# Mixer B's scores two chunks ahead of their transposes, and one run of six transposes divided in two

## The chip, the cores and the metric

The program runs on one core of a Trainium2 chip. The metric is the device time of one execution in microseconds. Three runs of the kernel before took 348.01, 349.36 and 349.63 us (median 349.36). The profile comes from a further execution of 348.68 us; its span, from the first instruction to the last, is 346.9 us. TensorE is called PE below, VectorE DVE, ScalarE ACT, GpSimd POOL.

## The reference, cut to what matters

One layer of a decoder trunk over 256 positions of 1024 channels, in float32. `h = rmsnorm(x)`; one wide product `h @ w_in` gives queries, keys and values of three mixers, their SiLU gates and the merge logits. The three mixers are

- A: eight heads; dilated causal windows in three groups, weighted by their softmax denominators;
- B: eight heads of block-sparse attention (one block at this length, so plain causal attention with a linear bias);
- M: four heads of attention to 256 memory tokens.

```python
p_a = (o_a * jax.nn.silu(a_gate)) @ w_branch_a[l]
p_b = (o_b * jax.nn.silu(b_gate)) @ w_branch_b[l]
p_m = (o_m * jax.nn.silu(m_gate)) @ w_branch_m[l]
g_a, g_b, g_m = jnp.split(jax.nn.sigmoid(merge_logits + b_merge[l]), N_BRANCHES, axis=-1)
merged = g_a * p_a + g_b * p_b + g_m * p_m
x = x + merged @ w_out[l]
```

and the result is `rmsnorm(x)` once more. The change touches the order of the attention work of mixers A and B, and no value.

## The kernel before

**Weight chunks.** `PLAN` lists 54 chunks of weights, numbered `i` from 0. The main loop takes them in turn. Chunk `i` is loaded three chunks ahead (L85), and two chunks ahead it is split into a high and a low part: ACT casts it to `wh` (L93), DVE subtracts to get `wl` (L94), each in two halves. A chunk's product has two halves of 24 matmuls of 128x128 by 256 columns: `wh` with the high and the low part of h (L232, L233), then `wl` (L235). Value chunks have the operands the other way round (L252 to L254). The result lands in a bank `pj`, and ACT or DVE takes it out.

**Attention steps.** Each mixer handles two heads (a pair) in steps. For mixer B (`pair_steps_b`) they are `scores` (eight matmuls into two banks `sb`, L296 and L297; then, for each head, a POOL multiplication for the bias table, two DVE scans L306 that add the bias and find the extreme, two exponentials on ACT, L312, and on DVE reciprocals L313 and normalisations L314), `trans` (six transposes on PE, three for each head, L320, and one ACT copy a head from `pt` to `ptsb`, L321), and `pv` (eight matmuls L449, then the gate). For mixer A (`pair_steps_a`) they are `first`, `second` (which holds the first six transposes), `trans(1)` (the other six) and `pv` (L409, L416).

**Where a step falls.** `chain` gives each step a slot and a sort key; `pump(i, 0)` runs what is due between the two halves of chunk `i`, `pump(i, 1)` behind the second half, so slot `2i` is the middle of chunk `i` and slot `2i+1` its end. Steps of one pair stand two slots (one chunk) apart. In mixer B pair n has its scores at slot 24+2n, transposes at 26+2n, `pv` at 28+2n. In one slot the order is: a `pv`, then scores, then transposes. Chunk 11 is the memory query, 12 the memory keys (its result `Mk` is taken out by DVE, L655, and split by ACT, `Mk12y`, L283 and L284), 13 the memory values, 14 and on mixer A. In mixer A the last pair (3) has its steps at slots 68, 70, 72 and 74; slot 72 holds its last six transposes alone, in the middle of chunk 36, and slot 74 its `pv`, in the middle of chunk 37. No attention step follows.

**What sets the order.** From chunk 8 on PE runs in the order of the code. The other engines' orders are fixed beforehand by a planner that works with simulated times; on the chip every engine then runs its own list in that fixed order, and an instruction that waits holds up all behind it.

**Buffers that the change meets.** Two score banks (`s`), two transposing banks (`pt`), four tiles `u` for the weights of the softmax (two a pair), three tiles `ptsb`, two tiles `nb` for the bias tables, two `wl`, three `wh`, three `pj`.

Of the kernel before, what the change touches and what calls it, by code (L numbers as in the profile page):

```python
# [63 lines left out]
def kernel(ctx: ExitStack, tc: tile.TileContext, wts: bass.AP, xT_d: bass.AP, memT_d: bass.AP,  # L64
# [47 lines left out]
    par, xT = xp[:, 0:40], xp[:, 40:].rearrange("p (k t) -> p k t", k=KD)  # L112
    for i in range(2):
        raws[i] = wp.tile([P, 2048], F32, tag="wraw", name=f"wraw{i}")
        src0 = wts[offs[i]:offs[i + 1]].rearrange("(p c) -> p c", p=P)
        for j in range(4):
# [3 lines left out]
            n = 512 if k else S  # L120
# [173 lines left out]
    def score(out, xs, yz, s, f, qs, ks):  # L294

        nc.tensor.matmul(out, xs[s][:, f, qs], yz[s][:, f, ks], start=True, stop=False)  # L296
        nc.tensor.matmul(out, xs[s][:, f, qs], yz[2 + s][:, f, ks], start=False, stop=True)  # L297

    qkv, gate, og, steps, ths, acc = {}, {}, {}, [], {}, {}
# [3 lines left out]
    def softmax(ps, tab, u, lo, hi):  # L303
        st = tp.tile([P, 4], F32, tag="st", name="st", bufs=12)
        if tab is not None:
            nc.vector.tensor_tensor_reduce(u[:, lo:hi], ps[:, lo:hi], tab, scale=1.0, scalar=3e38, op0=ALU.add,  # L306
                                           op1=ALU.min, accum_out=st[:, 0:1])
            src = u
        else:
            nc.vector.tensor_reduce(st[:, 0:1], ps[:, lo:hi], axis=mybir.AxisListType.X, op=ALU.min)  # L310
            src = ps
        nc.scalar.activation(u[:, lo:hi], src[:, lo:hi], AF.Exp, bias=st[:, 0:1], scale=-1.0, accum_out=st[:, 1:2])  # L312
        nc.vector.reciprocal(st[:, 2:3], st[:, 1:2])  # L313
        nc.vector.tensor_scalar(u[:, lo:hi], u[:, lo:hi], st[:, 2:3], None, op0=ALU.mult)  # L314

    def transposes(u, order, dst):

        ps = pa.tile([P, 512], F32, tag="pt", name="pt")
        for j, c in enumerate(order):
            nc.tensor.transpose(ps[:, P * j:P * (j + 1)], u[:, P * c:P * (c + 1)], ident)  # L320
        nc.scalar.copy(dst, ps[:, :P * len(order)].rearrange("p (j q) -> p j q", q=P))  # L321
# [21 lines left out]
    def pair_steps_a(pair):  # L343
        hf, f = pair // 2, pair % 2
        us, pts, nbs = {}, {}, {}

        def view(n, g):
            return qkv["A" + n, hf, g].rearrange("p (f t) -> p f t", f=2)

        def banks(par):  # L350
            if par == 0:
                for s in range(2):
                    nbs[s] = tp.tile([P, 512], F32, tag="nb", name="nba")
                    nc.gpsimd.tensor_scalar(nbs[s], tab_a, SLOPES_A[2 * pair + s], 1.0, op0=ALU.mult, op1=ALU.mult)  # L354
            return [pa.tile([P, 512], F32, tag="s", name="sa") for _ in range(2)]

        def near(ps, par):

            for s in range(2):
                if par == 0:  # L360
                    out = ps[s].rearrange("p (a b) -> p a b", a=2)[:, :, 0:P]
                else:
                    out = ps[s][:, 0:S]
                score(out, qkv["Aq", hf, 0], qkv["Ak", hf, 0], s, f, slice(P * par, P * (par + 1)), slice(0, S))

        def far(ps, par):

            for g in range(1, 3):
                for s in range(2):
                    rows = slice(HD * s, HD * (s + 1))  # L370
                    for r in range(2):
                        ts = slice(P * par + 64 * r, P * par + 64 * (r + 1))
                        lo = P * (par + 1) + 64 * (g - 1)
                        nc.tensor.matmul(ps[s][64 * r:64 * (r + 1), lo:lo + 64], view("q", g)[rows, f, ts],
                                         view("k", g)[rows, f, ts], start=True, stop=True)

        def weigh(ps, par):
            for s in range(2):
                us[s, par] = tp.tile([P, 512], F32, tag="u", name="u", bufs=4)
                softmax(ps[s], nbs[s][:, P * (1 - par):P * (4 - par)], us[s, par], 0, 384)  # L380

        def first():
            ps = banks(0)
            near(ps, 0)
            far(ps, 0)
            weigh(ps, 0)

        def second():

            ps = banks(1)  # L390
            far(ps, 1)
            trans(0)
            near(ps, 1)
            weigh(ps, 1)

        def trans(par):
            for s in range(2):
                if par == 0:
                    pts[s] = tp.tile([P, 3, 2, P], F32, tag="ptsb", name="ptsb", bufs=3)
                transposes(us[s, par], (0, 2, 1) if par == 0 else (0, 1, 2), pts[s][:, :, par, :])  # L400

        def pv():
            o = pa.tile([P, 512], F32, tag="o", name="oa", bufs=1)
            v0 = qkv["Av", hf, 0].rearrange("p (e c) -> p e c", e=2)
            vs = stacked[hf]
            for j in range(2):
                for s in range(2):
                    cols = slice(HD * (2 * f + s), HD * (2 * f + s + 1))
                    nc.tensor.matmul(o[HD * s:HD * (s + 1), 0:S], v0[:, j, cols],  # L409
                                     pts[s][:, j].rearrange("p e q -> p (e q)"), start=(j == 0), stop=False)  # L410
            for par in range(2):
                for r in range(2):
                    for s in range(2):
                        cols = slice(HD * (2 * f + s), HD * (2 * f + s + 1))
                        lo = P * par + 64 * r
                        nc.tensor.matmul(o[HD * s:HD * (s + 1), lo:lo + 64], vs[:, par, r, cols],  # L416
                                         pts[s][:, 2, par, 64 * r:64 * (r + 1)], start=False, stop=(par == 1 and r == 1))
            gated(o, "a", pair, False)

        return [first, second, lambda: trans(1), pv]  # L420

    def pair_steps_b(pair):
        hf, f = pair // 2, pair % 2
        us, pts = {}, {}

        def scores():
            banks = [pa.tile([P, 512], F32, tag="s", name="sb") for _ in range(2)]
            for lo, qs, ks in ((0, slice(P, S), slice(0, S)), (S, slice(0, P), slice(0, P))):
                for s in range(2):
                    score(banks[s][:, lo:lo + ks.stop], qkv["Bqx", hf], qkv["Bkx", hf], s, f, qs, ks)  # L430
            for s in range(2):
                nb = tp.tile([P, 512], F32, tag="nb", name="nbb")
                nc.gpsimd.tensor_scalar(nb[:, :S], tab_b, SLOPES_B[2 * pair + s], 1.0, op0=ALU.mult, op1=ALU.mult)
                us[s] = tp.tile([P, 512], F32, tag="u", name="u", bufs=4)
                softmax(banks[s], nb[:, 0:S], us[s], 0, S)
                softmax(banks[s], nb[:, P:S], us[s], S, S + P)

        def trans():
            for s in range(2):
                pts[s] = tp.tile([P, 4, P], F32, tag="ptsb", name="ptsb", bufs=3)  # L440
                transposes(us[s], (2, 0, 1), pts[s][:, 0:3])

        def pv():
            v = qkv["Bv", hf].rearrange("p (t c) -> p t c", t=2)
            o = pa.tile([P, 512], F32, tag="o", name="ob", bufs=1)
            for kt in range(2):
                for s in range(2):
                    cols = slice(HD * (2 * f + s), HD * (2 * f + s + 1))
                    nc.tensor.matmul(o[HD * s:HD * (s + 1), P * kt:S], v[:, kt, cols],  # L449
                                     pts[s][:, 2 * kt:2 + kt].rearrange("p j q -> p (j q)"), start=(kt == 0),  # L450
                                     stop=(kt == 1))
            gated(o, "b", pair, True)

        return [scores, trans, pv]
# [34 lines left out]
        while steps and steps[0][0] <= 2 * i + slot:  # L489
            steps.pop(0)[2]()  # L490

    def chain(pairs, first, each):

        for n, fns in enumerate(pairs):
            for j, fn in enumerate(fns):
                steps.append((first + each * n + 2 * j, (j + 1) % len(fns), fn))
        steps.sort(key=lambda z: z[:2])

    def out_mm(kc, wi, t):
# [75 lines left out]
    for i, (kind, key, src, col) in enumerate(PLAN):  # L575
# [73 lines left out]
        elif kind in ("Aq", "Ak", "Av", "Mq", "Mk", "Mv"):  # L649
            at = (kind,) + (key if kind[0] == "A" else (0,))  # L650
# [81 lines left out]
                if kc == 3:  # L732
                    finish(t)
        if kind == "Bv" and key == 1:
            chain([pair_steps_b(p) for p in range(4)], 2 * i + 14, 2)
        elif kind == "Mv":
            chain([pair_steps_m(p) for p in range(2)], 2 * i + 10, 2)
        elif kind == "Av" and key[1] == 0:
            chain([pair_steps_a(2 * key[0] + p) for p in range(2)], 2 * i + 2, 4)
# [68 lines left out]
```

## Time and profile before

| | before |
|---|---|
| runs | 348.01, 349.36, 349.63 us |
| profiled execution | 348.68 us |
| its span | 346.9 us |
| PE busy | 336.8 us (97%) |
| DVE busy | 233.3 us (67%) |
| ACT busy | 208.1 us (60%) |
| granted PE clock, mean | 0.994 of full |

A profile page gives the busy time of each engine, the chain of work that ended last, and the costliest groups of instructions. A view of waits says which engine sat idle for whom. A timeline lists single instructions: start, duration, engine, source line, operation, tiles. Matmuls are pipelined, so their durations overlap; the pace is read from the distance between starts. "The chain in order of time" gives the same without overlap: eight matmuls as one piece with the time that they really took.

### The profile page before, as it was taken

The numbers are of one execution on the slowest core, as the hardware profiler recorded it, in microseconds if no ns is written. First come the engines' busy times: TensorE is split into PE (matmuls) and PEld (weight loads), VectorE is DVE, ScalarE is ACT, GpSimd is POOL, SyncE is SP. The second block draws the span as 40 slices with busy tenths as digits, with TensorE's granted clock in tenths as the row PEclk, the third lists the DMA queues.
The fourth block names the chain that finished last, engine by engine and source line by source line (L and its number), as shares of the span: only waits on it lengthen the run. The fifth ranks groups of instructions, "written<-read, shape, count | busy, mean of one in ns | idle before, by whom it ended". The sixth has DMA issues, their size and how long they took to land.

```text
span 346.9 us, 7107 instructions
## 1 busy us (share of the span) xinstructions
PE 336.8 (97%) x2924; PEld 323.7 (93%) x2924; DVE 233.3 (67%) x402; ACT 208.1 (60%) x372; POOL 27.2 (8%) x40
## 2 busy tenths in 40 slices
PE   8999999998999999999999999999999999999992
PEld 5999999998999999999999999999999999999882
DVE  3859969899975666586665457677553755758553
ACT  6767767986865758575666356665515453645322
POOL 2402000001110000000110000000000412000022
PEclk9999999999999999999999999999999999999997
DMA  6998795955444444434533363543144547544003
GB/s 201 339 410 318 259 360 197 340 181 154 171 165 150 154 129 181 166 132 157 193 139 123 121 221 145 213 153 123 60 130 176 221 172 252 206 178 187 0 3 122
DMA packets 12945, 63.33 MB, mean 183 GB/s; under 512 B 1392, under 2 KB 2800, under 8 KB 6640
## 3 DMA queue, kind: packets, MB, share of 16 engines
q1 hardware_dynamic: 12912, 62.88, 50.6%
q8 instruction: 23, 0.38, 0.4%
q14 instruction: 10, 0.08, 0.1%
HBM read 61.82 MB, written 1.05 MB: 181 GB/s over the span
## 4 chain that ended last, share of the span: by engine, by line
PE 86%; DVE 4%; DMA 4%; SPq 2%; ACT 2%; issue 1%; POOL 0%; POOLq 0%; DVEq 0%
PE pj L232 16%; PE pj L235 16%; PE pj L233 16%; PE pj L252 5%; PE pj L254 4%; PE pj L253 4%; PE pt L320 3%; PE pw L232 3%; PE pw L233 3%; PE pw L235 3%; DMA xn<-in_x 2%; PE y L513 2%; PE y L514 2%; PE y L515 2%; DVE wl L94 2%; DMA wraw<-in_wts 1%
## 5 line engine op out<-in xcount | busy, mean ns | idle before, releaser
L94 DVE TENSOR_TENSOR wl<-wraw,wh 128x1024 fp32r<-128x1024 f32 (+2 forms) x117 | 129.5, 1143 | 56.3 <-issue 38.1
L93 ACT CAST wh<-wraw 128x1024 fp32r<-128x1024 f32 (+2 forms) x117 | 108.1, 968 | 48.7 <-PE pj L233 29.0
L232 PE MATMUL pj<-hh,wh 128*128 128x256 f32 x480 | 114.9, 281 | 0.0
L233 PE MATMUL pj<-hl,wh 128*128 128x256 f32 x480 | 114.1, 279 | 0.2 <-DVE hl L199 0.2
L232 PEld LDWEIGHTS pj<-hh,wh 128*128 128x128 f32 x480 | 90.4, 188 | 0.7 <-issue 0.6
L233 PEld LDWEIGHTS pj<-hl,wh 128*128 128x128 f32 x480 | 90.4, 188 | 0.4 <-DVE hl L199 0.4
L235 PE MATMUL pj<-hh,wl 128*128 128x256 f32 x480 | 65.2, 279 | 0.0
L235 PEld LDWEIGHTS pj<-hh,wl 128*128 128x128 f32 x480 | 59.8, 188 | 0.0
L252 PE MATMUL pj<-wh,hh 128*128 128x256 f32 x96 | 27.1, 283 | 0.0
L253 PE MATMUL pj<-wl,hh 128*128 128x256 f32 x96 | 26.7, 278 | 0.0
L254 PE MATMUL pj<-wh,hl 128*128 128x256 f32 x96 | 26.7, 278 | 0.0
L321 ACT COPY ptsb<-pt 128x384 f32<-128x384 f32 (+1 forms) x28 | 13.1, 493 | 14.7 <-PE pt L320 14.7
L312 ACT ACTIVATE u<-u,st 128x384 f32<-128x384 f32 (+2 forms) x32 | 17.0, 531 | 5.9 <-DVE st L306 5.8
L252 PEld LDWEIGHTS pj<-wh,hh 128*128 128x128 f32 x96 | 18.0, 188 | 0.1
L253 PEld LDWEIGHTS pj<-wl,hh 128*128 128x128 f32 x96 | 18.0, 188 | 0.0
L254 PEld LDWEIGHTS pj<-wh,hl 128*128 128x128 f32 x96 | 18.0, 188 | 0.0
L314 DVE TENSOR_SCALAR u<-u,st 128x256 f32<-128x256 f32 (+2 forms) x40 | 15.7, 398 | 1.0
L354 POOL TENSOR_SCALAR nba<-con 128x512 f32<-128x512 f32 x8 | 5.0, 622 | 125.4 <-DVE st L306 124.5
L320 PE MATMUL pt<-con,u 128*128 128x128 f32 x88 | 12.6, 279 | 1.5 <-DVE u L314 1.5
L514 PE MATMUL y<-wl,mgh 128*128 128x512 f32 (+1 forms) x40 | 13.9, 348 | 0.0
L513 PE MATMUL y<-wh,mgh 128*128 128x512 f32 (+1 forms) x40 | 13.9, 347 | 0.0
L515 PE MATMUL y<-wh,mgl 128*128 128x512 f32 (+1 forms) x40 | 13.9, 346 | 0.0
(195 smaller groups left out, 549.8 us busy)
## 6 DMA issues: line engine op xcount, KB each, us to landing
wraw<-in_wts SPq DMA_DIRECT2D x48, 1024.0 KB, 4.8
wraw<-in_wts SPq DMA_DIRECT2D x15, 256.0 KB, 5.9
xn<-in_x SPq DMA_DIRECT2D x1, 1024.0 KB, 8.2
memT<-in_memT SPq DMA_DIRECT2D x1, 1024.0 KB, 5.3
memn<-in_mem SPq DMA_DIRECT2D x1, 1024.0 KB, 7.9
xres<-in_xr SPq DMA_DIRECT2D x1, 1024.0 KB, 6.2
wraw<-in_wts SPq DMA_DIRECT2D x2, 512.0 KB, 3.2
out<-ysb SPq DMA_DIRECT2D x4, 256.0 KB, 2.0
```

What stands on the lines that cost most here:

```text
L93: nc.scalar.copy(whs[i][:, sl], raws[i][:, sl])
L94: lower[i] = nc.vector.tensor_tensor(wls[i][:, sl], raws[i][:, sl], whs[i][:, sl].bitcast(F32), op=ALU.subtract)
L232: nc.tensor.matmul(ps[:, lo:lo + S], wh[:, k, fs], ah[k], start=(k == 0), stop=False)
L233: nc.tensor.matmul(ps[:, lo:lo + S], wh[:, k, fs], al[k], start=False, stop=False)
L235: nc.tensor.matmul(ps[:, lo:lo + S], wl[:, k, fs], ah[k], start=False, stop=(k == kn - 1))
L252: nc.tensor.matmul(ps[:, lo:lo + S], ah[k], wh[:, k, :], start=(k == 0), stop=False)
L253: nc.tensor.matmul(ps[:, lo:lo + S], ah[k], wl[:, k, :], start=False, stop=False)
L254: nc.tensor.matmul(ps[:, lo:lo + S], al[k], wh[:, k, :], start=False, stop=(k == KD - 1))
L320: nc.tensor.transpose(ps[:, P * j:P * (j + 1)], u[:, P * c:P * (c + 1)], ident)
L513: nc.tensor.matmul(y[t, n][:, 0:w], ht, wh[:, k, cs], start=(kc == 0 and k == 0), stop=False)
L514: nc.tensor.matmul(y[t, n][:, 0:w], ht, wl[:, k, cs], start=False, stop=False)
L515: nc.tensor.matmul(y[t, n][:, 0:w], lt, wh[:, k, cs], start=False, stop=(kc == 3 and k == 1))
```

## The change

`chain` gets an argument `at` with the slots of a pair's steps. For mixer B it is (0, 4, 6) and the first slot is 22 instead of 24: pair n has its scores at 22+2n, and still its transposes at 26+2n and `pv` at 28+2n. So the four scores steps move up by one chunk (the first from the middle of chunk 12 to the middle of chunk 11, ahead of the small product `spread_m`, L181), and transposes and `pv` stay. In mixer A the last pair hands out five steps instead of four: its last transposes come as two steps of three, one for each head, at slot 72 (the middle of chunk 36) and slot 73 (the end of chunk 36); `pv` stays at 74. No instruction is added or removed.

```diff
-        def trans(par):
-            for s in range(2):
+        def trans(par, heads=(0, 1)):
+            for s in heads:
...
+        if pair == 3:
+            return [first, second, lambda: trans(1, (0,)), lambda: trans(1, (1,)), pv]
         return [first, second, lambda: trans(1), pv]
...
-    def chain(pairs, first, each):
+    def chain(pairs, first, each, at=(0, 2, 4, 6)):
 
         for n, fns in enumerate(pairs):
             for j, fn in enumerate(fns):
-                steps.append((first + each * n + 2 * j, (j + 1) % len(fns), fn))
+                slot = (0, 2, 4, 5, 6)[j] if len(fns) == 5 else at[j]
+                steps.append((first + each * n + slot, (j + 1) % len(fns), fn))
...
-            chain([pair_steps_b(p) for p in range(4)], 2 * i + 14, 2)
+            chain([pair_steps_b(p) for p in range(4)], 2 * i + 12, 2, (0, 4, 6))
```

## Rows read from the trace of the kernel before

**Rows 1.** The page: busy time of the engines.
```profile
PE 336.8 (97%) x2924; PEld 323.7 (93%) x2924; DVE 233.3 (67%) x402; ACT 208.1 (60%) x372; POOL 27.2 (8%) x40
```
**Rows 2.** The page: the chain that ended last, shares by engine.
```profile
PE 86%; DVE 4%; DMA 4%; SPq 2%; ACT 2%; issue 1%; POOL 0%; POOLq 0%; DVEq 0%
```
**Rows 3.** Waits of PE from 40 us on: total us, times, longest us.
```profile
PE pt L320 <- DVE u L314: 1.5, 1, 1.5
```
**Rows 4.** Timeline of PE, chunk 13: start us, us, instruction, count [idle before].
```profile
83.96 0.51 PE L320 MATMUL pt<-con,u 128*128 128x128 f32 x3
85.95 0.55 PE L320 MATMUL pt<-con,u 128*128 128x128 f32 x3 [1.47 <-DVE u L314]
86.25 0.36 PE L252 MATMUL pj<-wh,mh 128*128 128x256 f32 x1
```
**Rows 5.** Timeline of PE: scores in chunks 12 and 15, first `wl` product of 13, first pv.
```profile
76.69 0.28 PE L296 MATMUL sb<-Bk0y,Bq0x 128*128 128x256 f32 x1
...
77.57 0.33 PE L232 MATMUL pj<-mh,wh 128*128 128x256 f32 x1
...
80.48 0.28 PE L253 MATMUL pj<-wl,mh 128*128 128x256 f32 x1
...
91.98 0.44 PE L449 MATMUL ob<-ptsb,Bv 128*64 128x256 f32 x2
...
100.79 0.39 PE L296 MATMUL sb<-Bk1y,Bq1x 128*128 128x256 f32 x1
...
101.77 0.84 PE L320 MATMUL pt<-con,u 128*128 128x128 f32 x6
102.37 0.36 PE L232 MATMUL pj<-hh,wh 128*128 128x256 f32 x1
```
**Rows 6.** Timeline of DVE from 76 to 86 us, in its order.
```profile
76.18 2.35 DVE L94 TENSOR_TENSOR wl<-wraw,wh 128x1024 fp32r<-128x1024 f32 x2
...
79.28 0.42 DVE L306 CUSTOM_DVE_ANT_0 u<-sb,nbb 128x256 f32<-128x256 f32 x1
...
80.51 0.69 DVE L272 SCALAR_TENSOR_TENSOR Mq11x<-pj,Mq11x 64x512 fp32r<-64x512 f32 x1
...
81.97 2.34 DVE L94 TENSOR_TENSOR wl<-wraw,wh 128x1024 fp32r<-128x1024 f32 x2
84.34 0.69 DVE L655 TENSOR_TENSOR Mk<-pj,rb_m 128x512 f32<-128x512 f32 x1
...
85.27 0.41 DVE L306 CUSTOM_DVE_ANT_0 u<-sb,nbb 128x256 f32<-128x256 f32 x1
```
**Rows 7.** Timeline of ACT, chunk 13 and 14.
```profile
85.06 0.62 ACT L283 CAST Mk12y<-Mk 64x512 fp32r<-64x512 f32 x1 [1.41 <-DVE Mk L655]
...
89.52 0.46 ACT L321 COPY ptsb<-pt 128x384 f32<-128x384 f32 x1
```
**Rows 8.** Busy time in stretches: DVE is the third engine, clock behind POOL.
```profile
82.00:88.00 6.00, 4.53 (x41) 4.29 (x40) 5.96 (x17) 4.50 (x7) 1.12 (x2) 1.00 0.52 184
49.00:70.00 21.00, 21.00 (x188) 21.00 (x186) 19.19 (x30) 18.67 (x32) 0.71 (x1) 1.00 0.79 295
256.00:318.00 62.00, 62.00 (x528) 62.00 (x528) 36.89 (x38) 29.84 (x44) 7.00 (x4) 1.00 0.52 187
```
**Rows 9.** The chain in order of time: eight matmuls around two attention steps.
```profile
114.53 0.91 PE pj L235 x8
...
118.32 0.94 PE pj L235 x8
...
244.39 0.91 PE pj L235 x8
...
247.84 0.94 PE pj L235 x8
```
**Rows 10.** Timeline of ACT, chunk 36 to 37.
```profile
247.87 2.00 ACT L93 CAST wh<-wraw 128x1024 fp32r<-128x1024 f32 x2 [1.35 <-PE pj L233]
249.78 0.82 ACT L687 ACTIVATE thl<-pj,small 128x256 f32<-128x256 f32 x2
```

## The prediction, before the changed kernel ran

> **What bounds the kernel now.** First the busy times on the page: PE works 336.8 of the span's 346.9 us, DVE 67%, ACT 60% [rows 1]. Then the chain that ended last: 86% of it is PE's own work [rows 2]. So the time is the sum of PE's instructions, PE's waits, and a start and an end that this change does not touch. Only PE's waits and PE's pace can give anything. The view of waits names one PE wait behind the start that is worth the name: 1.5 us, once, transposes of L320 for a normalisation of L314 on DVE [rows 3]. The timeline places it: in chunk 13 the first pair of mixer B transposes its first head at 83.96, and the second head's three transposes come only at 85.95, 1.47 us late [rows 4]. The timeline of DVE shows why. The scans of that pair ran at 79.28, one head was normalised by 81.97, and then 2.34 us of `wl` and 0.69 us of `Mk` stood ahead of the second head's normalisation [rows 6]. DVE has no slack there: it is busy 5.96 of the 6 us from 82 to 88 [rows 8]. That matters below: what is put ahead in DVE's list delays what follows one for one.
>
> The pace is the second thing. PE's products of 128x256 columns run at two paces, eight in 0.91 or in 0.94 us [rows 9], in long unbroken stretches. The clock is not the reason: it is granted in full (1.00) both at 49 to 70 us, at the quick pace, and at 256 to 318 us, at the slow one [rows 8].
>
> **Part one: mixer B's scores one chunk earlier.** The eight score matmuls of each pair stay, and PE does them at another place. Four steps at slots 24 to 30 become four at 22 to 28; so one stands newly in the middle of chunk 11 and one is gone from the middle of chunk 15. The new one is priced by its like in chunk 12: from 76.69 to 77.57, 0.88 us. The one that goes took from 100.79 to 101.77, 0.98 us, since it came behind a `pv` [rows 5]. Net -0.10. From chunk 11 to chunk 15 PE thus runs 0.88 us later than now, less whatever wait goes.
>
> The wait: the first pair's scans now have their scores 0.88 us plus a chunk, some 6 us, earlier. To be late again, the second head's normalisation would have to slip beyond 84.84 (83.96 plus 0.88), three places behind where even the first head's ends now (81.97). I take the wait as gone. The run of six then costs what the undisturbed run of chunk 15 takes, 101.77 to 102.37, 0.60 us, in place of 83.96 to 86.25, 2.29 us [rows 4, 5]: -1.69. If the wait stays, 0; that is a rival below.
>
> What is late next? Each pair's scans take 1.23 us on DVE (79.28 to 80.51) and a head's normalising about 0.77 (81.20 to 81.97) [rows 6], so one pair more, up to 2.8 us, stands ahead of each other piece of DVE work from chunk 11 on, until mixer B's last pair. The pieces that PE waits for:
> - `wl` of chunk 13 ends at 78.53 [rows 6] and is first read at 80.48 [rows 5], which becomes 81.36. With the whole pair ahead of it, 81.3: just in time. Bounds 0 and 0.3; I take 0.
> - `wl` of chunk 14 ends at 84.31 [rows 6], and is read some 1.9 us into chunk 14, beyond 90: 0.
> - The two copies `ptsb` that the first `pv` needs. ACT makes the second at 89.52 to 89.98, behind `Mk12y`, which waits 1.41 us for DVE's `Mk` at 85.06 [rows 7]. The `pv` at 91.98 [rows 5] moves to 91.17, so the cover is 1.19 us. If `Mk` slips by 1.8 us (scans and one head) to 2.8, the `pv` waits 0.6 to 1.6. If the planner keeps `Mk` where it is, or puts the copies ahead of `Mk12y`, 0. I take 0, the nearer to the copies' place now, with a rival for the rest.
> - POOL's bias tables, the four tiles `u` and the score banks are freed in the same sequence as now; the third pair's scans must only wait until the first pair's transposes are through, which stand right behind its scores. No DMA is moved.
>
> **Part two: three and three.** Six transposes stay six. An interruption of PE's stream for them costs nothing that the rows show: a run of six takes 0.60 us, 0.10 for each. The copies for the second head move from behind 245.7 to behind the end of chunk 36, some 2.9 us before `pv`. On ACT a cast (247.87 to 249.87) and a tanh (249.78 to 250.60) may stand ahead of it [rows 10]; the copy then ends near 251.1 and `pv`, at about 251.5, still finds it. Bounds: 0 and 0.5 us of a wait; I take 0. On the other side stands the pace. Around the six lone transposes it changes from 0.91 (244.39) to 0.94 (247.84) [rows 9]. If a run of three leaves it quick, the 48 matmuls up to `pv` gain about 4.5 ns each, 0.2 us. But `pv` comes next, and behind a `pv` straight followed by a product the pace was slow even where it had been quick before: 114.53 quick, 118.32 slow [rows 9]. So I expect the long tail at the slow pace as now, and 0 for part two.
>
> The page "TensorE: Matmul & The Clock Gate" of the Trainium skill (section "Back-to-back issue gap") gives the gap of two matmuls as a function of the columns alone, 262 cycles for 256. By that rule there is one pace, no order of the steps can change it, and part two is worth exactly 0. The trace differs: the same shape at the same granted clock took 0.91 and 0.94 us for eight, so I keep the tail as a rival.
>
> **Sum.** -1.69 - 0.10 + 0 = -1.79 us. Against the profiled execution's 348.68 that is 346.9, against the median of 349.36 it is 347.6. The profile lies in the lower half of the runs; I start from the middle of both, 349.0, and forecast 347.2 us.
>
> **The rivals.**
> 1. *The tail turns quick.* If `pv`, reached from another pace and phase, hands on the quick pace, some 552 matmuls from there to 318 us gain. By the pieces of eight (0.94 less 0.91) that is 2.1 us, by the windows (62.0 us over 528 less 21.0 over 188) 3.1; I take 2.5: 344.7 us. For: the pace holds for long, and the last disturbance decides. Against: 118.32 above. Chance 0.13.
> 2. *The wait moves to the first `pv`.* `Mk` slips, `Mk12y` holds ACT, the copies are late, 0.6 to 1.6 us: 348.2 us. For: DVE is full, and ACT already waited 1.41 us for `Mk` [rows 7]. Chance 0.22.
> 3. *Nothing changes.* The planner puts the second head's normalisation behind the same `wl` and `Mk`, and only the 0.10 is left: 348.9 us. Against: 6 us of room. Chance 0.08.
> 4. *Slower: score banks.* The third pair's scores now stand ahead of the first pair's transposes, and need both banks empty at 83.96; that is, the second pair's scans must be done. Those scans stand behind `wl` and `Mk` now, at 85.27 [rows 6]. If the planner leaves them there while 0.77 us more stands ahead, they end at about 87.3, and PE waits 3.3 us where it waited 1.47: 349.0 - 1.8 + 3.3 = 350.5 us. It is slower from the point where the scans end after 85.75. Against: the scores come a chunk earlier, and the scans in the place of that chunk ended at 80.5 now. Chance 0.15.
>
> **How the numbers follow.** My forecast has 0.42, its own range 346.2 to 348.2 (the bounds on `wl`, on `pv` and on the 0.2 us of pace). To leave no more than 2 in 10 out, the range takes in rivals 1 to 3 and the lower edge of rival 4: 344.5 to 349.6. A measurement of this kernel tells about 0.5% from no change, 1.75 us: below 347.6 is faster, above 351.1 slower. Faster: two thirds of the forecast (0.28), rival 1 (0.13), a little of rival 2 (0.03): 0.44. Slower: a third of rival 4 (0.05) and 0.02 for what I don't see: 0.07. The rest, 0.49, is no change.
>
> **What the changed profile would show.** Right: the view of PE's waits has no wait of L320 for L314, the first run of six lasts 0.6 us, the scores stand at about 70.8 us, ahead of `spread_m`, and eight matmuls past 256 us take 0.94 us. Wrong: a wait of L449 for ACT's copy (rival 2), of L296 for DVE's scans (rival 4), of L320 as before (rival 3), or 0.91 us in the tail (rival 1). A wait of L409 near 250 us would refute the 0 of part two.

## The result, and the profile after

The changed kernel took 345.34 us (median of six, 345.19 to 346.32) beside 349.30 us before (six, 348.01 to 349.63): 0.9901 of the time, interval 0.9881 to 0.9921. The profiled execution after took 345.24 us, its span is 343.5 us. The forecast was 347.2 us, its range 344.5 to 349.6: the range holds the time, the forecast is 1.9 us too high.

The page of the profile after, busy times and the chain's shares by engine. Beside [rows 1, 2]: PE has 2.3 us less work with the same 2924 instructions, and its share of the chain rose from 86 to 90%.

```profile
PE 334.5 (97%) x2924; PEld 321.6 (94%) x2924; DVE 231.9 (68%) x402; ACT 208.3 (61%) x372; POOL 27.2 (8%) x40
...
PE 90%; DMA 5%; DVE 1%; ACT 1%; SPq 1%; issue 0%; POOL 0%; POOLq 0%; DVEq 0%
```

Waits of PE after, over the whole span (us in total, times, longest). All three lie in the start; the wait of L320 for L314 [rows 3] is gone.

```profile
PE pwarm L137 <- DVE zero L108: 1.0, 1, 1.0
PE pj L232 <- ACT wh L93: 0.9, 1, 0.9
PE pj L245 <- ACT wh L93: 0.5, 1, 0.5
```

Timeline of PE after: the first pair's scores in chunk 11, the third pair's in chunk 13, the first run of six, the product behind it, and the first `pv` (L451 here, L449 before). The six now take 0.59 us, 85.75 to 86.34, where they took 2.29 [rows 4].

```profile
71.65 0.28 PE L296 MATMUL sb<-Bk0y,Bq0x 128*128 128x256 f32 x1
...
84.87 0.28 PE L296 MATMUL sb<-Bk1y,Bq1x 128*128 128x256 f32 x1
...
85.75 0.84 PE L320 MATMUL pt<-con,u 128*128 128x128 f32 x6
86.34 0.37 PE L252 MATMUL pj<-wh,mh 128*128 128x256 f32 x1
...
92.09 0.65 PE L451 MATMUL ob<-ptsb,Bv 128*64 128x256 f32 x4
```

Timeline of DVE after [rows 6 before]: the first pair's scans, the normalisations of both heads, then `wl` and `Mk`. Both heads are ready at 83.65, 2.1 us ahead of their transposes. `Mk` stands at 86.06, straight behind the `wl` of chunk 14, as before.

```profile
75.43 0.42 DVE L306 CUSTOM_DVE_ANT_0 u<-sb,nbb 128x256 f32<-128x256 f32 x1
...
81.62 0.98 DVE L314 TENSOR_SCALAR u<-u,st 128x256 f32<-128x256 f32 x3
...
83.36 0.29 DVE L314 TENSOR_SCALAR u<-u,st 128x128 f32<-128x128 f32 x1
...
83.69 2.34 DVE L94 TENSOR_TENSOR wl<-wraw,wh 128x1024 fp32r<-128x1024 f32 x2
86.06 0.69 DVE L658 TENSOR_TENSOR Mk<-pj,rb_m 128x512 f32<-128x512 f32 x1
```

Timeline of ACT after [rows 7, 10 before]: the two copies for the first `pv`, and in chunk 37 the copy for mixer A's second head. The first pair is ready at 89.70 for a `pv` at 92.09, the last at 249.77 for one at 250.60.

```profile
86.30 0.48 ACT L321 COPY ptsb<-pt 128x384 f32<-128x384 f32 x1 [1.59 <-PE pt L320]
...
89.23 0.47 ACT L321 COPY ptsb<-pt 128x384 f32<-128x384 f32 x1
...
249.29 0.48 ACT L321 COPY ptsb<-pt 128x384 f32<-128x384 f32 x1
```

The chain in order of time after [rows 9 before]: eight products before the first run of three, between the two, then the last `pv`, and eight products in the tail. From 243 us to the first matmul into `y` no 0.94 stands.

```profile
243.56 0.91 PE pj L235 x8
244.47 0.33 PE pt L320 x3
...
246.62 0.91 PE pj L235 x8
247.53 0.33 PE pt L320 x3
...
250.60 1.01 PE oa L409 x8
...
256.82 0.91 PE pj L235 x8
```

The same 56 us of the tail in both kernels, busy times and granted clock (1.00, behind POOL); first after, then before. PE does 497 matmuls there instead of 477, 112.7 ns each instead of 117.4.

```profile
256.00:312.00 56.00, 56.00 (x497) 56.00 (x496) 34.23 (x35) 28.26 (x40) 7.01 (x4) 1.00 0.56 198
```

```profile
256.00:312.00 56.00, 56.00 (x477) 56.00 (x477) 32.83 (x33) 26.61 (x39) 7.00 (x4) 1.00 0.52 186
```

Where the time went is read best from five marks on PE's timeline: the first product of chunk 11, the first behind mixer B's last `pv`, the first of mixer A's last lone transposes, the first product behind the last `pv`, and the first matmul into `y`. All kernels of this study are in the table (us, one profiled execution each). The six stretches add up to the span; the execution is about 1.8 us longer.

| | to chunk 11 | to end of B | to lone transposes | to behind last `pv` | tail to `y` | rest | execution |
|---|---|---|---|---|---|---|---|
| before | 68.07 | 48.10 | 128.96 | 7.88 | 65.12 | 28.76 | 348.68 |
| after | 68.93 | 46.41 | 128.96 | 7.70 | 62.68 | 28.77 | 345.24 |
| e1, part one alone | 70.44 | 46.41 | 128.96 | 7.88 | 65.12 | 28.76 | 349.35 |
| e2, part two alone | 68.99 | 47.31 | 128.96 | 7.70 | 62.68 | 28.75 | 346.17 |
| e3, six at end of 36 | 70.20 | 46.52 | 131.68 | 5.05 | 65.12 | 28.77 | 349.16 |
| e4, a run of eight | 70.12 | 46.52 | 128.96 | 8.10 | 65.12 | 28.76 | 349.35 |
| d1, before, PE later | 69.58 | 46.62 | 128.96 | 7.88 | 65.12 | 28.75 | 348.73 |
| d2, after, PE later | 70.60 | 46.52 | 128.96 | 7.70 | 62.68 | 28.76 | 347.01 |
| e5, two and four | 69.51 | 46.41 | 128.96 | 7.70 | 62.68 | 28.76 | 345.82 |
| e6, pair 1 divided too | 68.59 | 46.41 | 128.88 | 7.70 | 62.68 | 28.76 | 344.81 |
| f1, one and five | 68.43 | 46.41 | 128.96 | 7.71 | 62.68 | 28.76 | 344.74 |
| f2, five and one | 68.27 | 46.41 | 128.96 | 7.71 | 62.68 | 28.76 | 344.57 |
| g1, six, then one again | 69.71 | 47.31 | 128.96 | 8.00 | 65.12 | 28.78 | 349.65 |
| g2, one again behind `pv` | 69.13 | 47.11 | 128.96 | 7.88 | 65.23 | 28.76 | 348.86 |

After less before: -1.69 in the second column (part one), -0.18 and -2.44 in the fourth and fifth (part two), +0.86 in the first, in a stretch that no edit touches and that differs from execution to execution. The rest is the same to 0.01 us.

### The profile page after: what moved, and what is told of

It reads as the page before. It is cut to its first block, busy times and chain, and to the rows that moved or that the text cites. A ratio compares the mean times of both kernels' runs of the same rounds, so it can differ in the third digit from the quotient of the medians.

```text
span 343.5 us, 7104 instructions
## 1 busy us (share of the span) xinstructions
PE 334.5 (97%) x2924; PEld 321.6 (94%) x2924; DVE 231.9 (68%) x402; ACT 208.3 (61%) x372; POOL 27.2 (8%) x40
## 4 chain that ended last, share of the span: by engine, by line
PE 90%; DMA 5%; DVE 1%; ACT 1%; SPq 1%; issue 0%; POOL 0%; POOLq 0%; DVEq 0%
PE pj L232 17%; PE pj L235 17%; PE pj L233 17%; PE pj L252 5%; PE pj L253 5%; PE pj L254 5%; PE pt L320 3%; DMA xn<-in_x 3%; PE pw L232 3%; PE pw L233 3%; PE pw L235 3%; PE y L517 2%; PE y L516 2%; PE y L518 2%; DMA xp<-in_xT 1%; PE oa L409 1%
## 5 line engine op out<-in xcount | busy, mean ns | idle before, releaser
L93 ACT CAST wh<-wraw 128x1024 fp32r<-128x1024 f32 (+2 forms) x117 | 108.1, 968 | 47.0 <-PE pj L233 27.7
L232 PE MATMUL pj<-hh,wh 128*128 128x256 f32 x480 | 113.9, 280 | 0.0
L232 PEld LDWEIGHTS pj<-hh,wh 128*128 128x128 f32 x480 | 90.2, 188 | 0.7 <-issue 0.6
L252 PE MATMUL pj<-wh,hh 128*128 128x256 f32 x96 | 27.1, 282 | 0.0
L254 PE MATMUL pj<-wh,hl 128*128 128x256 f32 x96 | 26.7, 278 | 0.0
L252 PEld LDWEIGHTS pj<-wh,hh 128*128 128x128 f32 x96 | 18.0, 188 | 0.1
L254 PEld LDWEIGHTS pj<-wh,hl 128*128 128x128 f32 x96 | 18.0, 188 | 0.0
L314 DVE TENSOR_SCALAR u<-u,st 128x256 f32<-128x256 f32 (+2 forms) x40 | 15.3, 398 | 0.8
L306 DVE CUSTOM_DVE_ANT_0 u<-sa,nba 128x384 f32<-128x384 f32 x16 | 8.3, 555 | 6.8 <-PE sa L297 3.8
```

The lines of the kernel that those rows point to most:

```text
L93: nc.scalar.copy(whs[i][:, sl], raws[i][:, sl])
L232: nc.tensor.matmul(ps[:, lo:lo + S], wh[:, k, fs], ah[k], start=(k == 0), stop=False)
L252: nc.tensor.matmul(ps[:, lo:lo + S], ah[k], wh[:, k, :], start=(k == 0), stop=False)
L254: nc.tensor.matmul(ps[:, lo:lo + S], al[k], wh[:, k, :], start=False, stop=(k == KD - 1))
```

## The experiments

**e1 and e2: each part alone.** Both edits are against the changed kernel. e1 leaves the last pair its four steps; e2 leaves mixer B its slots.

```diff
 e1
-        if pair == 3:
-            return [first, second, lambda: trans(1, (0,)), lambda: trans(1, (1,)), pv]
 e2
-            chain([pair_steps_b(p) for p in range(4)], 2 * i + 12, 2, (0, 4, 6))
+            chain([pair_steps_b(p) for p in range(4)], 2 * i + 14, 2)
```

> Part one alone: mixer B's scores two chunks ahead, the last six transposes of mixer A stay one run. Theory 'two separate gains' (part one removes the wait, part two turns the tail quick): no wait of L320 for L314, 1.7 us less than before at 115 us of the span, 0.94 us for eight matmuls past 256 us, 347.5 us against 349.3. Theory 'accident of timing' (the pace of the tail is drawn anew whenever anything upstream moves, part two has no part in it): the tail may come out quick here too, 0.91 us for eight and 345.2 us.

> Part two alone: the last six transposes in two runs of three, mixer B's scores as before. Theory 'two separate gains': the wait of 1.47 us stays, eight matmuls past 256 us take 0.91 us, 2.6 us less than before: 346.8 us. Theory 'accident of timing': the tail stays at 0.94 us as often as not; then 349.2 us.

Measured: e1 348.27 us beside 349.05 before, ratio 0.9987 (0.9971 to 1.0003); e2 346.26 us, ratio 0.993 (0.991 to 0.995). Part two is most of the gain, and part one by itself cannot be told from no change. e2's time came out near its forecast, but the wait of 1.47 us that was expected to stay was 0.47 us. Chain of e1, then of e2: behind six together the pace is slow from 248.52 on and stays so; behind three and three it is quick.

```profile
245.07 0.91 PE pj L235 x8
245.98 0.66 PE pt L320 x6
248.52 0.94 PE pj L235 x8
...
258.68 0.94 PE pj L235 x8
```

```profile
247.58 0.91 PE pj L235 x8
248.49 0.33 PE pt L320 x3
...
257.78 0.91 PE pj L235 x8
```

Timeline of PE in e2, chunk 13, with the old order of mixer B: the wait is 0.47 us, not 1.47 [rows 4].

```profile
85.86 0.55 PE L320 MATMUL pt<-con,u 128*128 128x128 f32 x3 [0.47 <-DVE u L314]
```

The other 1.0 us has its source earlier, in the execution that was profiled before. There a cast of weights on ACT (L93) waited for a DMA that brought the weights, and began 10.58 us ahead of chunk 11; in e2, g1 and g2, which have the same order on DVE, it waited for PE and began 11.59 us ahead. DVE follows ACT: its `wl` at 81.97 [rows 6] stands 13.90 us behind the start of chunk 11, in the other three 12.89 to 12.90. Timeline of ACT before, then in e2:

```profile
57.49 2.00 ACT L93 CAST wh<-wraw 128x1024 fp32r<-128x1024 f32 x2 [2.12 <-DMA wraw<-in_wts]
```

```profile
57.40 2.00 ACT L93 CAST wh<-wraw 128x1024 fp32r<-128x1024 f32 x2 [1.11 <-PE pj L233]
```

**e3 and e4: the place, or the run.** Both are the changed kernel but for mixer A's last transposes: e3 does all six at the end of chunk 36, e4 does eight together in the middle of chunk 36 (one of each head is done twice, into a part of the bank that nothing reads). Both also take the two lines for pair 3 out again.

```diff
 e3
...
-                slot = (0, 2, 4, 5, 6)[j] if len(fns) == 5 else at[j]
+                slot = at[j] + (first + each * n == 68 and j == 2)
 e4
...
-        for j, c in enumerate(order):
+        for j, c in enumerate(order + more):
...
+                           (0,) if pair == 3 and par == 1 else ())
...
```

> Changed kernel, but the last six transposes stay one run and move as a whole to the end of chunk 36 (slot 73). Theory 'length' (a lone run of six hands on the slow pace, one of three the quick one, and pv hands on the pace that it found): 0.94 us for eight behind it and in the whole tail, 347.6 us. Theory 'place' (what counts is that transposes stand at the end of chunk 36): 0.91 us and 345.3 us.

> Changed kernel, but the last transposes stay one run in the middle of chunk 36, and two transposes are done twice (the copies ignore them), so that the lone run has eight. Theory 'shortness' (a long lone run costs the pace, a short one doesn't): slow tail, 0.94 us for eight, 347.8 us. Theory 'phase' (each transposition shifts the stream by some ns against the weight loads, and what counts is where the run leaves it; lengths that are not three may come out quick too): 0.91 us and 345.6 us would be its sign, a slow tail would not refute it.

Measured: e3 347.91 us, ratio 0.9971 (0.9954 to 0.9987); e4 348.92 us, 0.9991 (0.997 to 1.0012). Chain of e3, then of e4: the pace is quick up to the run and slow behind it, at either place and for either length (four products in 0.47 us are the slow pace, in 0.45 the quick one). So it isn't slot 73 that helps. The tail takes 65.12 us in both. e4's median lies 1.1 us above its forecast of 347.8; no run explains that.

```profile
247.66 0.91 PE pj L235 x8
248.56 0.66 PE pt L320 x6
250.16 0.47 PE pw L235 x4
```

```profile
244.85 0.91 PE pj L235 x8
245.75 0.87 PE pt L320 x8
248.51 0.94 PE pj L235 x8
```

**d1 and d2: does the wait take up a delay of PE?** The kernels before and after, with the first product of chunk 9 done nine times more (about 1.02 us, started over each time, so nothing is added to the sum). `again` is a new argument of `mm_feat`.

```diff
...
+        for _ in range(again):
+            nc.tensor.matmul(ps[:, lo:lo + S], wh[:, 0, fs], ah[0], start=True, stop=True)
...
-                    mm_feat(ps, S * n, i, KD, S, n, ah, al)
+                    mm_feat(ps, S * n, i, KD, S, n, ah, al, 9 if (i, n) == (9, 0) else 0)
```

> Kernel before with PE made later on purpose: nine matmuls of 128x256 done again at the start of chunk 9 (nine times 113 ns, 1.02 us). Theory 'the wait takes up lateness' (the wait of the transposes is set by DVE's list, which does not move with PE, so that PE's lateness and the wait add up to the same): the wait shrinks by what is added, from 1.47 or 0.5 us to 0 to 0.5, and the time stays within 0.5 us of before, 349.1 to 349.6 us. Theory 'a wait of its own' (it comes on top whatever PE does before): 1.02 us more than before, 350.1 us.

> Changed kernel with the same nine matmuls done again at the start of chunk 9. Without the wait nothing takes the lateness up, by both theories: 1.02 us more than the changed kernel, 346.4 us against 345.3, and a quick tail (0.91 us for eight) all the same.

Measured: d1 349.43 us beside 348.98, ratio 1.0013 (0.9994 to 1.0031), +0.45 us for 1.02 us of work; d2 346.41 us, 0.992 (0.989 to 0.995), +1.07 over the changed kernel's 345.34 (which was measured apart from it). The interval of d1 reaches from -0.2 to +1.1 us and that of d2 (beside the kernel before) is wider, so the medians don't answer the question. Nor does the trace. In d1 the six transposes run without a wait, but not because PE is late: the planner, which works with simulated times of the edited kernel, fixed another order for DVE. Both heads of the first pair are now normalised ahead of the `wl` of chunk 14, where before one stood behind it and behind `Mk` [rows 6]. So whether the old order absorbs a delay of PE stays untested. What the pair does show is that the tail keeps its pace, slow in d1 and quick in d2, when PE comes later. Timeline of PE, then of DVE in d1 (L322 is L320 of the kernel before, L316 is L314):

```profile
85.46 0.84 PE L322 MATMUL pt<-con,u 128*128 128x128 f32 x6
```

```profile
81.80 0.53 DVE L316 TENSOR_SCALAR u<-u,st 128x256 f32<-128x256 f32 x2
82.25 2.35 DVE L94 TENSOR_TENSOR wl<-wraw,wh 128x1024 fp32r<-128x1024 f32 x2
```

**e5, f1 and f2: other divisions of the six.** The changed kernel with runs of two and four, one and five, five and one; shown is the edit of f1, and that of e5 is of the same kind.

```diff
 f1 (f2: 5 for 1)
-            return [first, second, lambda: trans(1, (0,)), lambda: trans(1, (1,)), pv]
+            def run(lo, hi):
+                for m in range(lo, hi):
+                    h, c = divmod(m, 3)
+                    if c == 0:
+                        pts["open"] = pa.tile([P, 512], F32, tag="pt", name="pt")
+                    ps = pts["open"]
+                    nc.tensor.transpose(ps[:, P * c:P * (c + 1)], us[h, 1][:, P * c:P * (c + 1)], ident)
+                    if c == 2:
+                        nc.scalar.copy(pts[h][:, :, 1, :], ps[:, :3 * P].rearrange("p (j q) -> p j q", q=P))
+            return [first, second, lambda: run(0, 1), lambda: run(1, 6), pv]
```

> Changed kernel, but the last six transposes come as two at slot 72 and four at slot 73. Theory 'phase by length' (what a lone run hands on depends on its length alone, and three gives quick, six and eight slow): the pace behind two and behind four shows on which side they lie; the tail then has the pace that stands behind four, since pv hands on what it finds: 345.3 us or 347.8. Theory 'shortness': both quick.

> The changed kernel, with its last six transposes divided into a run of one and a run of five. So far runs of two, three and four of these transposes, each between two products, were followed by the quick pace, runs of six and of eight by the slow one. Theory 'the length of the run decides': the run of one is followed by the quick pace; five is not bounded, and the tail goes with it: quick (0.91 us for eight matmuls past 256 us, stretch from the last pv to the first y matmul 62.68 us) or slow (0.94 and 65.12). Theory 'the division alone is enough, whatever the lengths': quick, 62.68 us, an execution of 345.2 to 345.9 us. A slow tail costs 2.4 us: 347.7 to 348.3.

> The same with a run of five first and a run of one at the end of chunk 36. Theory 'the length of the run decides, and the last one hands its pace on': the pace behind the five is the same as behind the five of the kernel with one and five; behind the single transpose it is quick whatever it was before, since runs of six behind a quick pace and pairs of three both set the pace anew; the tail is quick, 62.68 us, 345.2 to 345.9 us. Rival 'a short run only leaves the pace as it found it': if the five turn the pace slow, the single one leaves it slow and the tail takes 65.12 us, 347.7 to 348.3 us; if the five leave it quick, the two can't be told apart.

Measured, one execution each: 345.82, 344.74 and 344.57 us; the tail takes 62.68 us in all three. e5 lies within the spread of the changed kernel (345.19 to 346.32), f1 and f2 lie 0.45 and 0.62 us below it. The table puts that ahead of chunk 11: they reach it at 68.43 and 68.27, the changed kernel at 68.93. Chain of e5 and of f1: behind two and behind five the pace is as quick as in front of them.

```profile
244.15 0.91 PE pj L235 x8
245.06 0.22 PE pt L424 x2
247.11 0.91 PE pj L235 x8
```

```profile
245.92 0.91 PE pj L235 x8
246.83 0.55 PE pt L427 x5
248.30 0.45 PE pw L235 x4
```

**g1 and g2: does a short run set the quick pace, or keep what it finds?** The kernel before, its six together, and one of them done a second time, unread: at the end of chunk 36 (g1), or behind the last `pv`, at the end of chunk 37 (g2, whose edit has 7 for the 5 in the last line).

```diff
+        def again():
+            ps = pa.tile([P, 512], F32, tag="pt", name="pt")
+            nc.tensor.transpose(ps[:, 0:P], us[0, 1][:, 0:P], ident)
+        if pair == 3:
+            return [first, second, lambda: trans(1), pv, again]
...
-                steps.append((first + each * n + 2 * j, (j + 1) % len(fns), fn))
+                steps.append((first + each * n + (2 * j if j < 4 else 5), (j + 1) % len(fns), fn))
```

> The kernel before, with its six lone transposes together as they are, and one of them done a second time (unread) at the end of chunk 36. Runs of one to five, entered at the quick pace, were followed by the quick pace; runs of six and eight by the slow one. Open is whether a short run sets the quick pace or only keeps what it finds. Behind the six the pace is slow (0.94 us for eight). Theory 'a short run sets the quick pace': behind the single transpose it is quick, the last pv hands it on, and the tail from behind the last pv to the first y matmul takes 62.68 us: some 2.4 us off the kernel before, 346.3 to 347.2 us. Theory 'a short run keeps what it finds': slow behind it, the tail 65.12 us, and the execution as before plus 0.1, 348.7 to 349.8 us.

> The kernel before, with one transpose done a second time (unread) at the end of chunk 37, behind the last pv, where the pace is slow. Theory 'a short run sets the quick pace': the 24 matmuls from the pv to it are slow, all behind it quick: the stretch from behind the last pv to the first y matmul takes 62.68 plus some 0.1 (24 times 4.5 ns) plus 0.1 for the transpose itself, 62.9 us; 346.4 to 347.3 us. Theory 'a short run keeps what it finds': 65.12 plus 0.1, 65.2 us; 348.7 to 349.8 us.

Measured: 349.65 and 348.86 us (one execution each, the kernel before beside them 348.48). It keeps what it finds. Chain of g1: six turn the pace slow, the single one behind 248.68 + 0.95 leaves it slow, `pv` hands it on. In g2 it is 0.94 on both sides too.

```profile
246.14 0.66 PE pt L320 x6
248.68 0.95 PE pj L235 x8
...
258.95 0.94 PE pj L235 x8
```

**e6: the same for another pair.** The changed kernel with pair 1's last transposes divided as well; its second run of three falls in front of a value chunk (L252 to L254).

```diff
-        if pair == 3:
+        if pair in (1, 3):
```

> Changed kernel with the second pair's last six transposes (slot 54) divided in the same way, three and three. Theory 'the pace is handed on by fixed rules' (three hand on quick, pv hands on what it finds, the step from a value chunk to the next chunk turns quick into slow and slow into quick): quick from 185 to 195 us of the span, where it was slow, but slow from there to about 212 us, where it was quick; 0.2 us slower than the changed kernel, 345.5 us. Theory 'short runs are better everywhere': 11 us more at the quick pace and the rest as it was, 0.4 us faster, 344.9 us.

Measured: 345.06 us (344.53 to 346.81), ratio to before 0.9896 (0.986 to 0.9931); from the changed kernel's 345.34 it can't be told apart. Both forecasts missed: the stretch that holds it went from 128.96 to 128.88. Chain of e6: the first run of three keeps the quick pace where the six that stand there in the other thirteen kernels turn it slow, and half a chunk gains the 0.1 us; behind the second the value chunk starts slow, 0.12 a matmul. In the timeline of the changed kernel the value products behind runs of six and eight are slow as well (mostly 117 to 119 ns from start to start, from 86.34, 108.80, 129.47 and 170.54 on), so in front of a value chunk this short run did not help.

```profile
184.60 0.33 PE pt L320 x3
186.76 0.91 PE pj L235 x8
187.67 0.33 PE pt L320 x3
187.99 0.12 PE pj L252
```

## Why the prediction was right in one part and wrong in the other

**Base.** The middle of 348.68 and 349.36, 349.0, agrees with every later median of several runs of the kernel before (348.98 to 349.30).

**Part one, mechanism.** Right by each of its signs. The wait of L320 is gone, the run of six takes 0.59 us (0.60 forecast), the stretch from chunk 11 to mixer B's last `pv` is 1.69 us shorter (1.79 forecast), and e1 shows the same 46.41 with part one alone. The zeros held: no wait for `wl` and none for the copies. The planner put the first pair's scans ahead of the `wl` of chunk 13 (which ends at 79.50 and is first read at about 82.3), and nearly all of both heads' work ahead of the `wl` of chunk 14, so that no normalising of the first pair is left behind `Mk`.

**Part one, size.** 1.69 us is what it gave against the one execution that I read. In the median it gave 0.78 (349.05 less 348.27, a ratio whose interval reaches 1), or 0.92 (e2's 346.26 less 345.34). e3 and e4, which hold part one too, lie 1.14 and 0.13 us below before, so the medians give its size only roughly. The reason is the wait itself. With the old order of mixer B it was 1.47 us in the execution profiled before, where weights landed late for ACT, and 0.47 to 0.48 in e2, g2 and g1, which have the same order on DVE and began chunk 11 at 68.99, 69.13 and 69.71: a PE that came 0.7 us later did not shorten it. From chunk 11 to the end of B these four took 48.10, 47.31, 47.11 and 47.31, which is 1.69, 0.90, 0.70 and 0.90 more than the new order's 46.41. (d1 had no wait and took 46.62, with the other order on DVE.) So the term of -1.69 for the wait was the size of one execution, not of the kernel; I corrected the base from that execution to the median by 0.3 us and left the term as it was.

**Part two.** This is the step that failed: "So I expect the long tail at the slow pace as now, and 0 for part two". The first half of the thought was right. A run of three does leave the pace quick, and the stretch up to `pv` gains 0.18 us where the text gives 0.2. Wrong was the next sentence, which took what a `pv` of mixer B does (114.53 quick, 118.32 slow, [rows 9]) for what the last `pv` of mixer A would do. That one has other shapes (eight products of L409 and sixteen small ones of L416 in place of eight of L449), and it hands on the pace that it finds: quick to quick in after, e2, e5, f1 and f2, slow to slow in before, e1, e3, e4, g1 and g2. The trace before has no `pv` of this kind that is entered at the quick pace and followed straight by a product; the two ends should have been 0 and -2.5, with neither much likelier. The tail gained 2.44 us and the whole of part two 2.62, which was rival 1's price (2.5; its upper end, by the windows, comes to 3.2 and not 3.1), given 0.13.

The prediction took the 262 cycles for 256 columns as a rule for this stream. The section "Back-to-back issue gap" of the page "TensorE: Matmul & The Clock Gate" of the Trainium skill gives that formula for the isolated gap of a single matmul; of a stream of weight loads and matmuls, as this kernel has it, it says that both set the spacing, and it has no figure for 256 columns. Had one gap held for one count of columns, e1 and the changed kernel would have the same tail. They differ by 2.44 us with the same instructions in it, at a granted clock of 1.00: here the measurement decides.

**The other rivals.** 2: no wait of the first `pv`, the copies are there 2.4 us early; DVE reached `Mk` 1.7 us later than before (0.9 us, counted from the start of chunk 11), PE's first `pv` came 0.1 us later (0.7 us earlier, counted so), and ACT did the first copy ahead of `Mk12y` instead of waiting for `Mk`. 3: refuted by the second column. 4: the third pair's scores start at 84.87 with no wait of L296 on the list, so the banks were empty.

**The sum as it came.** Part one 0.8 to 0.9 and part two 2.6 make 3.4 to 3.5 us; the medians differ by 3.96, and the ratio's interval is 2.8 to 4.2 us. The rest is inside what the start and chunks 6 to 11 vary by. The forecast's own range, 346.2 to 348.2, missed; the wide range holds the time because rival 1 was taken into it. And there was luck in the 1.9 us: part one was put 0.9 us too high and part two 2.6 us too low, so that one error hid some of the other.

**What stays open.** Why a run of six or eight turns the pace slow in front of a product of L232 while one to five keep it, and why in other places of the changed kernel, straight behind a `pv`, six (101.10) and eight (136.31) are followed by the quick pace. From the start of the first product behind a run to the start of the second it is 0.20 to 0.21 us in all of them, which does not tell the two apart. The runs show the rule in chunk 36 and, for three and six, at pair 1's place (e6), both entered at the quick pace; not its cause.

## What to carry to other kernels

When PE is busy 97% of the span, look for its pace as well as its waits: count matmuls of one shape in equal windows at full granted clock, and find the instruction behind which the count changes. The last such place ahead of a long undisturbed stretch is worth its whole length; a few instructions there, divided in another way, gained more than the wait that the view of waits named. And price a wait from several executions: this one was 1.47 us in the first that was read, where weights came late for another engine, and 0.47 us in the next three. When an edit is meant to test one thing, compare the other engines' orders as well: in d1 the planner changed DVE's, and the wait went with it.

## What the runs showed of the hardware that was not expected

- TensorE issues the same stream (128x128 weights, 256 columns, float32 words) at two lasting paces, 0.91 and 0.94 us for eight, with the clock granted in full (1.00). In the stretches read it changed only where the stream was interrupted or passed between value chunks and the others.
- In chunk 36 runs of 1, 2, 3, 4 and 5 transposes kept the quick pace, 6 and 8 turned it slow; a single one kept the slow pace as well. Whether 2 to 5 keep the slow pace too was not tried.
- The pace also falls differently from execution to execution early in the span: from 49 to 67 us PE does 161 or 162 matmuls in eleven of the fourteen profiles, and 155 in e3, e4 and d2. In e3 and e4 the pace stays slow behind PE's stop in chunk 6 (0.88 and 0.45 us from start to start), where in the eleven a stop of 0.41 to 0.55 us is followed by the quick pace; d2 has no such stop and is slow from 26 us on. From chunk 6 to chunk 11 e3 took 1.4 us longer than the execution profiled before. No edit of e3, e4 or d2 lies ahead of that. The window of e3, at full clock:

```profile
49.00:67.00 18.00, 18.00 (x155) 18.00 (x154) 16.96 (x23) 16.36 (x28) 0.71 (x1) 1.00 0.73 274
```
